# TensorE's matmuls in the order of emission, and background steps every 4 matmuls, in a decoder step

## The chip, the cores and the metric

One core of a Trainium2 chip runs the whole program. The core has TensorE (matmuls; PE in the rows, PEld for its weight loads), VectorE (DVE), ScalarE (ACT), GpSimd (POOL), and SyncE (SP), which issues nearly all DMAs. [...] The metric is the device time of one execution in microseconds.

## The reference

One inference step of a one-layer decoder, for a prompt of 2048 tokens and 8 sample tokens with a cache of 2048 positions each. All arrays are float32.

```python
q, k, v, u = _project(rmsnorm(hp, norm_attn_g[i]), w_in[i])     # 1024 -> 4 x 512
for window, dil in ((128, 1), (512, 4), (2048, 16)):            # dilated windows, 8 heads of 64
    o, l = _dilated_attn_prompt(q, k, v, window, dil)
...
pooled = _pool_mix(u, S, pool_w[i], pool_scale[i])              # trailing means over 2, 4, 8, 16
hp = hp + _mixer_out(outs, lses, pooled, w_out[i])              # merge by exp(lse), then 1024 x 1024
hp = hp + _mlp(hp, norm_mlp_g[i], w_up[i], w_down[i])           # squared ReLU, 1024 -> 4096 -> 1024
hp = hp + _ple(hp, p_prompt[i], ple_norm_g[i], w_ple_gate[i], w_ple[i])
```

The same is computed for the sample tokens, whose attention reads the cache. The outputs are both token groups after a last RMSNorm, the new K and V rows, and the pooling buffers.

## The kernel before

Activations lie transposed, features on the partitions and tokens along the columns. Each dense product is made of groups: `group` (line 340) multiplies a chunk of up to 512 token columns by 128 output features, over 8 blocks of features, into one PSUM bank. Each operand is split into a high and a low part, and three products are summed (`PASSES`), so a group has 24 matmuls (6 in the per-layer embedding, more in the down projection). New weights come by DMA; POOL rounds the high part (`pcopy`, line 199) and DVE subtracts it for the low part (line 196).

The rest of the work, preparing inputs, attention, normalisation, is written as Python generators, called background. A group takes a `hook`; every 12 matmuls and at its end it reports the columns done to a `Pace`, which runs as many background steps as are then due. So instructions of the background are emitted between the matmuls of a group.

The stages, in order: input projection of the first 1024 tokens (columns of 512), while the second half's input is prepared; input projection of the rest (384, 384 and 264 columns) with the first half's attention as background (`Att(0, ...)`), which goes on beside the per-layer embedding product (`ple_mm`); then, for the first 832 tokens (X, chunks of 416), output projection and MLP with the second half's attention (`Att(1, ...)`) and the sample attention (`sample_attn`) as background; then output projection, MLP and gate of the other 1224 tokens (Y, chunks of 416, 416 and 392).

Attention goes head by head. `maxima` finds each query's maximum by masked reductions on DVE (line 776); `units` yields the work of a head in pieces. A unit is: scores into a bank, exponential on ACT (line 868 for the class units of the dilated windows, 871 for the near units of the plain window), two masks on POOL (line 859), a rounding on ACT (line 880), a subtraction on DVE (line 196), then the weighted sums with V. In `out` the sums of a unit are emitted one step after its scores, behind the scores of the next:

```python
for nxt, hold in self.units(h, ops, ov):
    if pend:
        pend()
    pend = nxt
    yield
```

`Stat.finish` sums squares by four one-column matmuls, takes the inverse square root on DVE and ACT (`newton`, line 306), and turns it with four transposes (line 1204). `sample_attn` reads the cache tile by tile; ACT rounds a V tile into one buffer (line 1107), DVE subtracts into another, and two matmuls use them.

The emission order is not the order on the engines. The program is built with `schedule_with_timeline_sim=True`: a scheduler runs a timeline of its own over all emitted instructions and places them on each engine as they come ready in it, earlier emitted ones first. So a matmul of one group can stand between matmuls of another.

Of the kernel before, what the change touches and what calls it, by code (L numbers as in the profile page):

```python
# [147 lines left out]
@with_exitstack  # L148
def decoder_step(ctx: ExitStack, tc: tile.TileContext, I, O):
    nc = tc.nc  # L150
    V, S, G, PE, SP = nc.vector, nc.scalar, nc.gpsimd, nc.tensor, nc.sync
    y_p, y_s, kv_p, kv_s, pool_p, pool_s = O

# [35 lines left out]
    def mm(out, l, r, start, stop):  # L189
        PE.matmul(out, l, r, start=start, stop=stop)  # L190
# [150 lines left out]
    def group(ps, ln, ws, xs, hook=None):  # L341

        n, last, due = 0, 3 * len(ws) - 1, 0
        for w, x in zip(ws, xs):
            for a, b in PASSES:
                mm(ps[:, :ln], w[:, a], x[:, b, :ln], n == 0, n == last)
                n += 1
                if hook and (n % 12 == 0 or n == last + 1):
                    hook((n - due) * ln)
                    due = n  # L350

# [231 lines left out]
    def in_proj(hf, xa, order, rg, mp, tp, hook, ws, first=None):  # L583
# [21 lines left out]
        for ft, ci in [(ft, ci) for ci in range(len(chunks)) for ft in order[:n0]] + [(ft, ci) for ft in order[n0:] for ci in range(len(chunks))]:  # L605
            if ft not in ws:
                ws[ft] = in_w(ft, rg["wr"])
            w, (c0, ln) = ws[ft], chunks[ci]
            if ci and first:
                drain(first)  # L610
                first = None
            ps = mp()
            group(ps, ln, [w[:, :, k] for k in range(KD)], xa.col(ci), first_hook if first else hook)
            now, later = later, []
            later += [x for x in [x() for x in now] if x]
            for o, e, n, lo in pieces(c0, ln):
                if n < 4:
                    if n not in open_:
                        open_[n] = rg["gt"]()
                    tt(V, open_[n][:, lo : lo + e - o], ps[:, o:e], rbc[n][:, lo : lo + e - o], ALU.mult)  # L620
                    if lo + e - o == 512:
                        rest = group_done(ft, n, open_.pop(n), rg, tp)
                        if rest:
                            later.append(rest)
                elif ft >= 12:
                    tt(V, us[:, ft - 12], ps[:, o:e], rbs, ALU.mult)
                    later.append(partial(pool_sample, ft - 12, rg, tp))
                else:
                    t = TINY(NS, key="in", n=2, width=NS)
                    tt(V, t, ps[:, o:e], rbs, ALU.mult)  # L630
                    later.append(sample(ft, t))
# [502 lines left out]
    def ple_mm(mp, tp, wr, pr, hook):  # L1134
# [13 lines left out]
        for c0, ln in ((0, 512), (512, 512), (1024, 512), (1536, 256), (1792, T - 1792)):  # L1148
            pp = pb().rearrange("p (k a c) -> p k a c", a=2, k=2)
            pt = []  # L1150
            for p0 in range(c0, min(c0 + ln, SEQ), 256):
                n, r = p0 // 512, p0 % 512 // P
                t = pr(512).rearrange("p (r d) -> p r d", r=2)
                dma(t, prows[n][:, r : r + 2])
                pt += [(t[:, 0], P), (t[:, 1], P)]
            if c0 + ln == T:
                t = pr(256)[:NS]
                dma(t, I["p_sample"][0].rearrange("b o d -> (b o) d"))
                pt.append((t, NS))
            for k in range(2):  # L1160
                ps = tp()
                for r, (t, rw) in enumerate(pt):
                    PE.transpose(ps[:, r * P : r * P + rw], t[:, k * P : k * P + P], ident[:rw, :rw])
                S.copy(pp[:, k, 0, :ln], ps[:, :ln])
                tt(V, pp[:, k, 1, :ln], ps[:, :ln], f(pp[:, k, 0, :ln]), ALU.subtract)
            for ft in range(KD):
                ps = mp()
                group(ps, ln, [w[ft // 4][:, k, :, (ft % 4) * P : (ft % 4) * P + P] for k in range(2)], [pp[:, k] for k in range(2)], hook)
                o = orr(ln)
                (S.copy if ft % 2 else V.tensor_copy)(o, ps[:, :ln])  # L1170
                dma(ple[ft * P : ft * P + P, c0 : c0 + ln], o)
# [111 lines left out]
    def out_proj(xa, st, dst, wr, hook, acc=None, ring=None):  # L1283
# [11 lines left out]
        for i, (ft, ci) in enumerate(order):  # L1295
            if ft not in ws:
                ws[ft] = load_w(I["w_out"][0][:, ft * P : ft * P + P], KD, wr=wr, ring=ring)
            w = ws[ft]
            c0, ln = chunks[ci]
            ps = mp()  # L1300
            at = (slice(ft * P, ft * P + P), slice(c0, c0 + ln))
            xr = acc[ft].ap[:, c0 - base : c0 - base + ln] if acc else xr_(ln)
            dma(xr, xT[at])
            group(ps, ln, [w[:, :, k] for k in CORDER], [xa[k, ci] for k in CORDER], None if acc and i >= len(order) - 4 else hook)
            tt(V, xr, ps[:, :ln], xr, ALU.add)
            if dst is not None:
                dma(dst[at], xr)
            st.add(ft, ci, xr)
            if done is not None:
                st.finish(done)  # L1310
                done = None
            if ft == KD - 1:
                done = ci
# [249 lines left out]
    hook = Pace(bg, A.steps(), 16 * 24 * 1032 + 0.6 * 48 * T)  # L1563
# [21 lines left out]
    hook = Pace(bg, B.steps(), 24 * NX * (8 + 64 * 0.9))  # L1585
# [122 lines left out]
```

## Time and profile before

| what | value |
|---|---|
| median of 3 runs | 2738.77 us (2737.43 to 2738.94) |
| profiled execution, own time | 2732.91 us |
| its span, first to last instruction | 2731.2 us |
| TensorE busy | 2651.1 us, 97% |
| TensorE weight loads busy | 2526.3 us, 92% |
| DVE, ACT, POOL busy | 57%, 31%, 38% |
| granted TensorE clock, mean | 0.991 |
| DMA, mean | 100 GB/s |

The spans of matmuls overlap, since they are pipelined; a busy TensorE is one that always has a matmul under way. [...]

### The profile page before, as it was taken

The numbers are of one execution on the slowest core, as the hardware profiler recorded it, in microseconds if no ns is written. First come the engines' busy times: TensorE is split into PE (matmuls) and PEld (weight loads), VectorE is DVE, ScalarE is ACT, GpSimd is POOL, SyncE is SP. The second block draws the span as 40 slices with busy tenths as digits, with TensorE's granted clock in tenths as the row PEclk, the third lists the DMA queues.
The fourth block names the chain that finished last, engine by engine and source line by source line (L and its number), as shares of the span: only waits on it lengthen the run. The fifth ranks groups of instructions, "written<-read, shape, count | busy, mean of one in ns | idle before, by whom it ended". The sixth has DMA issues, their size and how long they took to land. (4 is left out here: it accounts for less than half of the span.)

```text
span 2731.2 us, 43094 instructions
## 1 busy us (share of the span) xinstructions
PE 2651.1 (97%) x15686; PEld 2526.3 (92%) x15686; DVE 1559.9 (57%) x3373; ACT 846.6 (31%) x1605; POOL 1030.2 (38%) x1370
## 2 busy tenths in 40 slices
PE   8999999998999999999999898999999999999998
PEld 6888899978988999999999898999999999999997
DVE  6747867675587776775765857432332332332675
ACT  6221445463434134243343424301001011011354
POOL 2415745434385444343344626312112122122263
PEclk9999999999999999999999999999999999999999
DMA  7464345476154233342322545331111111111134
GB/s 248 133 180 124 86 121 136 110 224 177 49 150 113 81 88 82 97 107 71 99 73 66 167 142 149 127 104 39 42 41 42 39 39 39 39 39 39 53 84 150
DMA packets 386194, 272.51 MB, mean 100 GB/s; under 512 B 91722, under 2 KB 349461, under 8 KB 385973
## 3 DMA queue, kind: packets, MB, share of 16 engines
q1 hardware_dynamic: 385397, 269.68, 34.6%
q8 instruction: 123, 2.02, 0.3%
q14 instruction: 90, 0.74, 0.1%
q0 software_dynamic: 512, 0.07, 0.0%
q10 hardware_dynamic: 72, 0.02, 0.0%
HBM read 209.47 MB, written 60.30 MB: 99 GB/s over the span
## 5 line engine op out<-in xcount | busy, mean ns | idle before, releaser
L190 PE MATMUL bank<-mem_r 128*128 128x416 f32 (+11 forms) x13608 | 2454.0, 338 | 46.9 <-DVE mem_r L196 13.3
L190 PEld LDWEIGHTS bank<-mem_r 128*128 128x128 f32 (+2 forms) x13608 | 2307.9, 184 | 127.4 <-DVE mem_r L196 22.9
L199 POOL TENSOR_SCALAR mem_r<-mem_f 128x512 fp32r<-128x512 f32 (+1 forms) x444 | 325.2, 737 | 773.6 <-PE bank L190 689.1
L196 DVE TENSOR_TENSOR mem_r<-mem_f,mem_r 128x512 fp32r<-128x512 f32 (+3 forms) x568 | 435.5, 773 | 176.2 <-POOL mem_r L199 142.8
L196 DVE TENSOR_TENSOR mem_f<-bank,mem_f 128x416 f32<-128x416 f32 (+3 forms) x488 | 272.7, 566 | 234.5 <-PE bank L190 227.6
L196 DVE TENSOR_TENSOR mem_r<-mem_mb,mem_r 128x416 fp32r<-128x416 f32 (+6 forms) x236 | 174.0, 744 | 349.3 <-ACT mem_r L1347 318.3
L1344 ACT ACTIVATE mem_mb<-bank 128x392 f32<-128x392 f32 (+1 forms) x160 | 82.2, 514 | 801.0 <-PE bank L190 801.0
L196 POOL TENSOR_TENSOR mem_mb<-mem_mb 128x416 f32<-128x416 f32 (+1 forms) x140 | 143.7, 1027 | 304.2 <-ACT mem_mb L1344 277.9
L776 DVE CUSTOM_DVE_ANT_0 bank<-bank,mask 128x256 f32<-128x256 f32 (+3 forms) x504 | 159.8, 338 | 33.9 <-PE bank L190 30.1
L199 POOL TENSOR_SCALAR mem_r<-mem_r 128x256 fp32r<-128x256 f32 (+1 forms) x117 | 92.0, 798 | 92.2 <-PE bank L190 81.1
L196 DVE TENSOR_TENSOR mem_ma<-bank,mem_ma 128x416 f32<-128x416 f32 (+2 forms) x104 | 63.4, 610 | 87.5 <-PE bank L190 72.8
L1347 ACT CAST mem_r<-mem_mb 128x416 fp32r<-128x416 f32 (+1 forms) x128 | 68.5, 535 | 134.4 <-POOL mem_mb L196 134.4
L859 POOL TENSOR_SCALAR_AFFINE_SELECT mem_ma<-mem_ma 128x256 f32<-128x256 f32 (+2 forms) x148 | 72.0, 506 | 92.2 <-ACT mem_ma L871 49.3
L190 PE MATMUL bank<-mem_mb,mem_r 128*64 128x64 f32 (+4 forms) x494 | 100.7, 321 | 6.2 <-DVE mem_r L196 2.1
L190 PEld LDWEIGHTS bank<-mem_mb,mem_r 128*128 128x128 f32 (+1 forms) x494 | 78.7, 174 | 16.0 <-POOL mem_r L199 2.8
L196 DVE TENSOR_TENSOR mem_r<-mem_ma,mem_r 128x512 fp32r<-128x512 f32 (+4 forms) x88 | 71.6, 819 | 26.4 <-ACT mem_r L880 20.5
L199 POOL TENSOR_SCALAR mem_r<-mem_mb 128x512 fp32r<-128x512 f32 (+3 forms) x61 | 55.3, 913 | 79.4 <-PE bank L190 55.8
L196 POOL TENSOR_TENSOR mem_f<-mem_f 128x416 f32<-128x416 f32 (+2 forms) x52 | 70.0, 1351 | 31.3 <-DMA mem_f<-in_cache_attn_kv_dram 11.4
L776 DVE DVE_READ_ACCUMULATOR2_ANT mem_ma<- 128x1 f32 (+1 forms) x512 | 68.5, 134 | 0.0
L196 POOL TENSOR_TENSOR mem_ma<-mem_ma 128x416 f32<-128x416 f32 (+1 forms) x41 | 51.8, 1272 | 39.7 <-DMA mem_ma<-h_s 14.1
L196 DVE TENSOR_TENSOR mem_f<-mem_f,mem_ma 128x416 f32<-128x416 f32 (+1 forms) x64 | 46.9, 733 | 26.2 <-ACT mem_ma L1190 11.3
L859 POOL TENSOR_SCALAR_AFFINE_SELECT mem_mb<-mem_mb 128x256 f32<-128x256 f32 (+2 forms) x76 | 34.5, 474 | 57.9 <-ACT mem_mb L868 22.8
(255 smaller groups left out, 1807.7 us busy)
## 6 DMA issues: line engine op xcount, KB each, us to landing
mem_f<-in_w_up_dram SPq DMA_DIRECT2D x128, 256.0 KB
mem_f<-in_w_down_dram SPq DMA_DIRECT2D x128, 256.0 KB
mem_f<-in_w_in_dram SPq DMA_DIRECT2D x64, 256.0 KB
out_dram<-mem_f SPq DMA_DIRECT2D x55, 256.0 KB
mem_f<-in_cache_attn_kv_dram SPq DMA_DIRECT2D x48, 256.0 KB
mem_f<-in_w_ple_gate_dram SPq DMA_DIRECT2D x48, 256.0 KB
mem_f<-in_x_prompt_dram SPq DMA_DIRECT2D x64, 128.0 KB
xT_s<-mem_f SPq DMA_DIRECT2D x32, 256.0 KB
```

What stands on the lines that cost most here:

```text
L190: PE.matmul(out, l, r, start=start, stop=stop)
L196: eng.tensor_tensor(out, a, b, op=op)
L199: G.tensor_scalar(out, src, 1.0, 1.0, op0=ALU.mult, op1=ALU.mult)
L776: V.tensor_tensor_reduce(src, src, mask, 1.0, -3e38, ALU.add, ALU.max, mcol[: src.shape[0], col : col + 1])
L859: G.affine_select(out=p, in_=p, pattern=[[0, nblk], [sign, w]], compare_op=ALU.is_ge, fill=0.0, base=base, channel_multiplier=-sign)
L1344: S.activation(a, ps[:, :ln], AF.Relu)
L1347: S.copy(x[:, 0], sq)
```

## The change

```diff
@@ -148,6 +148,7 @@
 @with_exitstack
 def decoder_step(ctx: ExitStack, tc: tile.TileContext, I, O):
     nc = tc.nc
+    ctx.enter_context(tc.manual_schedule(engines={mybir.EngineType.PE}))
     V, S, G, PE, SP = nc.vector, nc.scalar, nc.gpsimd, nc.tensor, nc.sync
     y_p, y_s, kv_p, kv_s, pool_p, pool_s = O
 
@@ -345,7 +346,7 @@
             for a, b in PASSES:
                 mm(ps[:, :ln], w[:, a], x[:, b, :ln], n == 0, n == last)
                 n += 1
-                if hook and (n % 12 == 0 or n == last + 1):
+                if hook and (n % 4 == 0 or n == last + 1):
                     hook((n - due) * ln)
                     due = n
```

The first edit takes TensorE out of the scheduler's hands: its instructions stand in the order in which the kernel emits them. The other engines are still ordered by the scheduler. The second lets a group report after every 4 matmuls instead of 12, so that the steps due are emitted in smaller lots. All line numbers after the first edit are higher by one.

The order of TensorE's instructions in the two programs differs nearly everywhere. The rows below are TensorE's; `bank_70` to `bank_77` are the eight PSUM banks before, `bank_72` to `bank_79` the same eight after; 128x416 is the matmul's output, x6 the number of equal rows in a run.

First place: a near unit of the second half's attention, first of its head, in the MLP of X. Before, from its four score matmuls (128x256) to the first of its weighted sums (65x256):

```order
L190 MATMUL bank_75<-mem_r 128x256 x4
L190 MATMUL bank_77<-mem_ma_1831 65x64 x8
L190 MATMUL bank_72<-mem_r 128x416 x5
L190 MATMUL bank_70<-mem_r 128x416 x6
L190 MATMUL bank_71<-mem_r 128x416 x6
L190 MATMUL bank_75<-mem_r 128x256 x4
L190 MATMUL bank_73<-mem_r 128x416 x5
L190 MATMUL bank_76<-mem_r 65x256
```

The same unit now:

```order
L191 MATMUL bank_77<-mem_r 128x256 x4
L191 MATMUL bank_79<-mem_ma_1833 65x64 x8
L191 MATMUL bank_73<-mem_r 128x416 x6
L191 MATMUL bank_75<-mem_r 128x416 x4
L191 MATMUL bank_76<-mem_r 128x128 x2
L191 MATMUL bank_78<-mem_r 65x256
```

Between scores and sums stood 22 matmuls of 416 columns and the next unit's scores; now 10 of 416 and two of 128 columns. In the first half's attention the last near unit of a head stands closer still; here that of the fourth head, its scores (bank_77) and sums (bank_79), in the input projection:

```order
L191 MATMUL bank_77<-mem_r 128x256 x2
L191 MATMUL bank_77<-mem_r 128x128 x2
L191 MATMUL bank_73<-mem_r 128x384 x4
L191 MATMUL bank_79<-mem_r 65x256
L191 MATMUL bank_79<-mem_r 64x256
```

One lot of 4 matmuls stands between them. Second place: the weighted sums of one sample token over its three V tiles (16x512, two matmuls for a tile), in the MLP of X. Before:

```order
L190 MATMUL bank_74<-mem_r 16x512 x2
L190 MATMUL bank_71<-mem_r 128x416 x12
L190 MATMUL bank_73<-mem_r 128x416 x10
L190 MATMUL bank_74<-mem_r 16x512
L190 MATMUL bank_73<-mem_r 128x416 x9
L190 MATMUL bank_74<-mem_r 16x512
L190 MATMUL bank_73<-mem_r 128x416 x5
L190 MATMUL bank_75<-mem_r 64x128 x4
L190 MATMUL bank_72<-mem_r 128x416 x5
L190 MATMUL bank_74<-mem_r 16x512
```

And now:

```order
L191 MATMUL bank_72<-mem_r 128x416 x24
L191 MATMUL bank_73<-mem_r 128x416 x4
L191 MATMUL bank_76<-mem_r 16x512 x6
L191 MATMUL bank_73<-mem_r 128x416 x20
L191 MATMUL bank_75<-mem_r 128x416 x8
```

All six stand in one row. Third place: the sums of squares (104x1) and the transposes of the inverse root (128x104) of the first chunk of X, in the output projection. Before:

```order
L190 MATMUL bank_71<-mem_r 128x416 x6
L190 MATMUL bank_72<-ones_96,mem_f 104x1 x4
L190 MATMUL bank_71<-mem_r 128x416 x18
L190 MATMUL bank_73<-mem_r 128x416 x11
L1204 MATMUL bank_72<-ident_91,tiny_7140 128x104 x4
L190 MATMUL bank_73<-mem_r 128x416 x13
```

And now:

```order
L191 MATMUL bank_72<-mem_r 128x416 x24
L191 MATMUL bank_74<-ones_98,mem_f 104x1 x4
L1205 MATMUL bank_74<-ident_93,tiny_7142 128x104 x4
L191 MATMUL bank_73<-mem_r 128x416 x24
L191 MATMUL bank_75<-mem_r 128x416 x24
```

The transposes stood 29 matmuls behind the sums, and now follow them.

## Rows read from the trace of the kernel before

**Rows 1.** The page, part 1: busy us, share of the span and instructions of each engine.

```profile
PE 2651.1 (97%) x15686; PEld 2526.3 (92%) x15686; DVE 1559.9 (57%) x3373; ACT 846.6 (31%) x1605; POOL 1030.2 (38%) x1370
```

**Rows 2.** Waits of TensorE: line, releaser, us in total, times, longest.

```profile
PE bank L190 <- DVE mem_r L196: 15.4, 20, 2.3
PE bank L190 <- DVE mem_f L196: 11.4, 14, 2.9
PE bank L190 <- POOL mem_r L199: 10.8, 8, 2.8
...
PE bank L190 <- ACT mem_r L880: 6.3, 7, 2.4
```

**Rows 3.** Stretches: busy us (instructions) of PE, PEld, DVE, ACT, POOL; clock, DMA, GB/s.

```profile
273.10:341.40 68.30, 62.98 (x439) 58.24 (x440) 56.20 (x155) 28.04 (x52) 49.16 (x61) 0.90 0.32 86
409.70:478.00 68.30, 68.30 (x555) 65.87 (x554) 48.98 (x160) 35.31 (x67) 35.83 (x60) 1.00 0.57 136
614.50:682.80 68.30, 59.23 (x373) 54.74 (x371) 40.48 (x118) 23.65 (x44) 27.63 (x43) 0.90 0.65 177
1911.80:1980.10 68.30, 68.30 (x371) 67.82 (x370) 22.31 (x36) 5.75 (x11) 12.69 (x17) 1.00 0.14 42
```

**Rows 4.** Timeline, start and length in us: a near unit and, in between, the maxima's store.

```profile
449.59 1.11 ACT L871 ACTIVATE mem_ma<-bank 128x512 f32<-128x512 f32 x1
...
450.78 1.21 POOL L859 TENSOR_SCALAR_AFFINE_SELECT mem_ma<-mem_ma 128x256 f32<-128x256 f32 x2 [1.27 <-ACT mem_ma L871]
...
451.55 1.16 PE L190 MATMUL bank<-mem_f 64*65 64x64 f32 x16
...
451.68 1.42 SPq L187 DMA_DIRECT2D m_s<-mem_ma  x3
452.02 0.62 ACT L880 CAST mem_r<-mem_ma 128x512 fp32r<-128x512 f32 x1 [0.39 <-POOL mem_ma L859]
...
452.68 0.69 DVE L196 TENSOR_TENSOR mem_r<-mem_ma,mem_r 128x512 fp32r<-128x512 f32 x1
...
453.49 1.67 SPq L187 DMA_DIRECT2D mem_ma<-m_s  x4
```

**Rows 5.** Lines 868, 859 and 880: count, ns minimum/median/maximum, first and last start.

```profile
L868 ACT ACTIVATE mem_ma<-bank x32: 465/546/602, 277.2 to 1466.3; 128x384 f32<-128x384 f32 x16, 128x512 f32<-128x512 f32 x16
...
L859 POOL TENSOR_SCALAR_AFFINE_SELECT mem_ma<-mem_ma x148: 285/407/1651, 279.1 to 1490.6; 128x256 f32<-128x256 f32 x108, 128x128 f32<-128x128 f32 x24, 64x512 f32<-64x512 f32 x8, 128x512 f32<-128x512 f32 x8
...
L880 ACT CAST mem_r<-mem_ma x64: 510/617/647, 280.3 to 1491.0; 128x512 fp32r<-128x512 f32 x44, 128x384 fp32r<-128x384 f32 x20
```

**Rows 6.** Groups by line and shape, 888 to 1500 us: count | busy us, mean ns.

```profile
L196 DVE TENSOR_TENSOR mem_r<-mem_f,mem_r 128x512 fp32r<-128x512 f32 x127 | 99.5, 788 | 35.7 <-POOL mem_r L199 28.8 <-ACT mem_r L1107 2.7 <-ACT mem_r L880 2.3
...
L1107 ACT CAST mem_r<-mem_f 128x512 fp32r<-128x512 f32 x24 | 14.9, 620 | 44.2 <-PE bank L190 42.7 <-DVE mem_r L196 1.1 <-DMA mem_f<-in_cache_attn_kv_dram 0.4
```

**Rows 7.** Timeline around one finish of the row statistics.

```profile
717.38 0.81 PE L190 MATMUL bank<-ones,mem_f 128*104 128x1 f32 x8
...
720.45 0.16 DVE L196 TENSOR_TENSOR tiny<-tiny,tiny 104x4 f32<-104x4 f32 x1
...
723.62 0.52 PE L1204 MATMUL bank<-ident,tiny 104*128 104x104 f32 x4
```

**Rows 8.** Timeline of TensorE at the start, and the stretch from 10 to 20 us.

```profile
12.90 1.22 PE L190 MATMUL bank<-mem_ma,mem_r 128*128 128x512 f32 x2 [2.84 <-POOL mem_r L199]
...
21.07 1.77 PE L190 MATMUL bank<-mem_ma,mem_r 128*128 128x512 f32 x7
...
26.82 0.60 PE L464 MATMUL bank<-ident,rcols 128*128 128x128 f32 x4
...
10.00:20.00 10.00, 7.16 (x31) 5.56 (x30) 5.93 (x11) 7.51 (x24) 2.50 (x4) 1.00 1.00 316
```

**Rows 9.** Lines 776 and 572: count, ns minimum/median/maximum.

```profile
L776 DVE CUSTOM_DVE_ANT_0 bank<-bank,mask x504: 197/319/469, 232.6 to 1436.6; 128x256 f32<-128x256 f32 x74, 64x128 f32<-64x128 f32 x42, 64x64 f32<-64x64 f32 x37, 128x128 f32<-128x128 f32 x15
...
L572 ACT COPY mem_f<-bank x32: 559/587/652, 39.2 to 551.8; 128x512 f32<-128x512 f32 x32
```

## The prediction

> **What bounds the kernel now.** I read the page's first two parts first, then who TensorE waited for, then stretches of the span, and last the order of rows around the places where the change acts. TensorE is busy for 2651.1 of 2731.2 us [rows 1], so 80.1 us is all that it sits idle; DVE, ACT and POOL are at 57, 31 and 38%. The waits are scattered: 37.6 us of them, the first three rows [rows 2], are mostly for copies and subtractions of freshly loaded weights and for evacuations; waits for attention weights (line 880) come to 6.3 us in seven places. In the dense stretch after 1911.8 us, TensorE runs 371 matmuls of 408 columns on average in 68.3 us [rows 3]: 184 ns each, 0.45 ns a column. I use that price for every matmul of 128 columns or more, and 0.07 us for each of 64 (16 took 1.16 us [rows 4]). The slice from 409.7 us, full of attention and projection, has no idle time either. So before the change TensorE is the bound nearly everywhere, and the order that the scheduler chose hides nearly every chain through the other engines. The most that a better order could give is the 80.1 us and what the clock lost; the loss has no such bound.
>
> **The change, part by part.** No instruction is added or removed; both edits move some. The finer step (4 instead of 12 matmuls) changes where background steps are emitted; in itself it costs nothing, since the same steps come, about one or fewer at a time instead of up to three. The fixed order is what counts: a matmul that waits for ACT, POOL or DVE now holds all matmuls behind it, where before the scheduler put other groups ahead. So I count, at each place, the TensorE work that stands between a result's producer and its consumer (the cover), and set it against the chain through the other engines.
>
> *Attention units.* A unit is scores, exponential, two masks, a rounding, a subtraction, then weighted sums. In one near unit (lines 871 to 881) the exponential starts at 449.59 us, the subtraction ends at 453.37: 3.8 us with almost nothing in front [rows 4]. A class unit: 0.55 + 2 x 0.41 + 0.62 + 0.79, and four handovers of 0.05 to 0.1 us: 3.1 us [rows 5, 6]. The order gives the cover. Over the eight heads of the first half, the four near units had medians of 4.5, 7.1, 8.9 and 8.1 us of matmuls between scores and sums; now 3.2, 1.9, 1.4 and 0.7. In the second half 5.4 to 8.4 us become 2.7, 2.9, 2.4 and 2.1. Of 64 near units two had under 3.6 us, now 61 have. A stall ahead of one unit's sums is cover for the next one's whose scores are already issued. For a head of the first half: 3.8 - 3.2 = 0.6; 3.8 - 1.9 - 0.6 = 1.3; 3.8 - 1.4 - 1.3 = 1.1; the fourth unit's scores come after that, so 3.8 - 0.7 = 3.1: 6.1 us, eight times, 49. The second half: 1.1 + 0 + 1.4 + 1.7 = 4.2, eight times, 34. The same count over the 64 class units gives 10. In all 93 us. With one subtraction of 0.79 us queued in front (chains of 4.5 and 3.9) the same count gives 141. DVE is busy for 49 to 56 us of the 68.3 in such slices [rows 3], so there are gaps, and I stay nearer the lower end: 106 us.
>
> *Sample attention.* For each of eight samples three value tiles pass through one pair of buffers: rounding 0.62 us on ACT, subtraction 0.79 on DVE [rows 6], two matmuls of 0.23 us. The six matmuls stood 10 to 19 dense matmuls apart; now they stand in one row. So the second and third tile each cost about (0.62 + 0.07 - 0.23) + (0.79 + 0.07 - 0.23) = 1.1 us: 16 x 1.1 = 18. The third tile's buffer is refilled by a DMA only after the first is used; no row gives its landing. Lower bound 0; upper, from the store at 451.68 to its read-back at 453.49 us, 1.8 us [rows 4], plus 0.8 for 256 KB at the 316 GB/s of the start [rows 8]: 2.6. I take 1.4, as the subtraction of the second tile covers part: 8 x 1.4 = 11. Together 29.
>
> *Row statistics.* Ten times four sums go through ACT and DVE to four transposes: from the end of the sums at 718.19 us to that of the last DVE step at 720.61, 2.4 us [rows 7]. Some 29 matmuls stood between them, now none: 24 us. Four of the sums now also directly follow the last group whose evacuation, square and addition they need, three operations like those of [rows 5]; I put 1.5 us for what they add, since little else was left to do there before either: 6. Together 30.
>
> *The single transpose bank.* Some 16 transposes of new rows stand right behind others in the same bank and wait for its copy, 0.59 us [rows 9]: 10. Six pooling matmuls stand right behind a POOL copy and a DVE subtraction, about 1.5 us: 9. *Maxima.* The 16 transposes of a head's maxima follow the last reductions, two or more of some 0.32 us and their read-outs [rows 9], about 1.3 us; the cover is 0 to 2.8 us: 9, and 6 where scores wait for a bank. *Per-layer embedding.* Five chunks start with the rounding and subtraction of their own input: about 1.2 us each, 6.
>
> *The start.* Dense matmuls began at 12.9 us, while the statistic of the first rows was ready only for 26.82 us [rows 8]. Now 32 transposes and that statistic come first. 22 matmuls of 512 columns, some 5 us, had been issued by 22.7 us; with the later rows' transposes 6 us are lost. The DMA rate is the bound there, so no more.
>
> *What comes back.* While TensorE stands still the others run ahead: of the 37.6 us of [rows 2] I take back 20. Stalls of different kinds lie among each other: a quarter of the sample, bank and maxima terms, 16.
>
> *The clock.* [...] Attention now gets 8 to 10 us of idle time in each of some 17 slices: 0 to 116 us, of which I take 25, since matmuls at half clock are longer cover for the same chains. [...]
>
> Sum: 106 + 29 + 30 + 19 + 15 + 6 + 6 - 20 - 16 + 25 = 200 us. The profiled execution took 2732.91 us, 1.7 more than its span, and 0.2% under the median of 2738.77; added to the median, 2939, rounded to 2935 us.
>
> **The rivals.**
> *The clock falls in every slice.* For it: the two rows at 0.90; against it: slower matmuls hide more of each chain. With 90 instead of 25: about 3000 us.
> *The stalls hide one another.* Units, samples and statistics share a stretch, the other engines drain their queues in each stall, and what follows finds its input ready. With chains as short as 3.2 and 2.5 us the units cost 62, and half of the rest would remain: about 2850 us.
> *Faster.* Even steps keep the other engines evenly fed, and a fixed order uses results as soon as they stand; then weights come in time and idle time falls to about half: 40 us less, 2700 us. This decides at the near units: the cover has to reach 3.8 us, and the counted covers say 0.7 to 3.2.
> *The order does not bind.* Were TensorE to pass a waiting matmul, nothing would change: 2735 us. Against it: idle time with a single releaser, such as 15.4 us for line 196, while other groups stood behind [rows 2]. [...]
>
> **How the numbers follow.** Forecast (2890 to 2980): 0.46. Clock (2980 to 3060): 0.21. Hidden (2800 to 2890): 0.21. Faster: 0.06. No change: 0.03. Still slower than all: 0.03. Slower by over 0.2%, which is about what a measurement can tell from no change, is then 0.91, the same 0.03, faster 0.06. The range from 2820 to 3050 leaves out the last three and the edges.
>
> **What would show it.** In the profile after, TensorE's first waits should be for line 881 (ACT) and the subtraction of line 197, together 80 to 130 us, and the transposes of line 1205 should wait ten times, about 24 us. Slices in the first half's attention should hold 470 to 510 matmuls instead of 555; slices of the second half's MLP, with no background, should keep 371. The busy sums of DVE, ACT and POOL should stay within 2%. The prediction is wrong if the waits for lines 881 and 197 stay under 40 us, or if TensorE's idle time lies where weights are loaded.

## The result, and the profile after

The changed kernel takes 3078.74 us (median of 4 runs, 3075.49 to 3085.02), the kernel before, run beside it, 2738.86 us: 1.1258 of the time before, with an interval from 1.1243 to 1.1273. The forecast was 2935 us, its range ended at 3050. The direction was right, the size too small by 144 us.

Part 1 of the page after, and the digits of PE and PEclk from part 2 (busy tenths and granted clock in 40 slices):

```profile
span 3073.6 us, 43178 instructions
...
PE 2765.8 (90%) x15686; PEld 2607.6 (85%) x15686; DVE 1553.9 (51%) x3373; ACT 855.9 (28%) x1599; POOL 996.1 (32%) x1370
...
PE   7898688888788999998989959899999999999997
...
PEclk8998889988988999998999989999999999999998
```

Against [rows 1] two things grew, with not one matmul more. TensorE's idle time, span minus busy, went from 80.1 to 307.8 us: 227.7 more. Its busy time went from 2651.1 to 2765.8: 114.7 more, because the same matmuls ran longer. Together 342.4 us, which is the whole difference of the spans (3073.6 - 2731.2). The second part is nearly all the clock: its mean fell from 0.991 to 0.943. The trace's records hold two levels of it, 1.00 and 0.50 of full speed, so that is (1 - 0.943) x 2 x 3073.6 = 350 us at 0.50, where it was about 50 before. Some of that time TensorE was idle anyway. With the trace's records of the granted clock laid over its matmuls, TensorE is busy at the lower level for 255.9 us, against 39.9 before, in 55 stretches against 9. Half of the difference, 108 us of the 114.7, is taken as what the slow clock cost. That is an estimate with twice the time for each matmul at 0.50, and somewhat high: around 2026 us in the trace after, 128x416 matmuls start every 347 ns at 0.50 and every 190 ns at 1.00, so that 45% of their time is lost, which would make it 98 us.

TensorE's longest waits after (line, releaser, us in total, times, longest), to be read against [rows 2]:

```profile
PE bank L191 <- ACT mem_r L881: 77.2, 41, 5.7
PE bank L191 <- DVE mem_r L197: 43.7, 64, 3.1
PE bank L1205 <- DVE tiny L197: 29.5, 10, 7.1
PE bank L191 <- POOL mem_r L200: 26.1, 10, 6.0
PE bank L838 <- DVE mem_ma L777: 22.4, 11, 3.3
PE bank L191 <- DVE mem_f L197: 14.7, 11, 3.4
PE bank L191 <- POOL mem_f L197: 12.2, 1, 12.2
PE bank L465 <- DVE rcols L432: 10.7, 2, 7.1
```

Line 881, the rounding of attention weights, was 6.3 us in seven waits; it is now 77.2 in 41. The same idle time by the shape of the waiting matmul (count | busy us, mean ns | idle before, and what ended it):

```profile
L191 PE MATMUL bank<-mem_r 128*128 128x512 f32 x672 | 186.7, 422 | 35.8 <-POOL mem_r L200 23.0 <-DVE mem_r L197 11.0 <-ACT mem_r L1165 1.3
...
L191 PE MATMUL bank<-mem_r 128*65 128x256 f32 x320 | 91.4, 316 | 105.6 <-ACT mem_r L881 77.2 <-DVE mem_r L197 26.8
...
L191 PE MATMUL bank<-mem_r 128*16 128x512 f32 x48 | 20.8, 461 | 9.9 <-ACT mem_r L1108 5.7 <-DVE mem_r L197 3.7
...
L191 PE MATMUL bank<-ones,mem_f 128*104 128x1 f32 x64 | 8.1, 247 | 14.8 <-POOL mem_f L197 12.2 <-DVE mem_f L197 2.0 <-ACT mem_f L1206 0.7
...
L1205 PE MATMUL bank<-ident,tiny 104*128 104x104 f32 x32 | 6.1, 330 | 22.8 <-DVE tiny L197 22.8
...
L838 PE MATMUL bank<-ident,mem_ma 128*16 128x128 f32 x16 | 4.7, 295 | 22.6 <-DVE mem_ma L777 22.4
...
L1205 PE MATMUL bank<-ident,tiny 98*128 98x98 f32 x8 | 1.8, 384 | 6.6 <-DVE tiny L197 6.6
L191 PE MATMUL bank<-ones,mem_f 128*98 128x1 f32 x16 | 1.7, 228 | 4.7 <-DVE mem_f L197 4.7
```

This view gives one number for each of the larger terms of the prediction: the weighted sums of the attention (128x256 by 65 rows) wait 105.6 us, the maxima's transposes 22.6, the row statistics 22.8 + 6.6 + 14.8 + 4.7 = 48.9, the sample's V products 9.9. The 35.8 us at 128x512 are nearly all at the pooling's products: seven waits for POOL's rounding of the pooled means (23.0), most with one for the subtraction behind it. These are totals after. The attention's sums had 14.0 us in the kernel before, so the change added 92:

```profile
L190 PE MATMUL bank<-mem_r 128*65 128x256 f32 x320 | 85.3, 291 | 14.0 <-DVE mem_r L196 7.3 <-ACT mem_r L880 6.3
```

One such wait in the timeline (start and length in us; in brackets the idle time before and its releaser), the last near unit of a head in the first half:

```profile
363.57 1.51 PE L191 MATMUL bank<-mem_r 128*128 128x128 f32 x5
...
364.73 2.16 POOL L200 TENSOR_SCALAR mem_r<-mem_mb 128x256 fp32r<-128x256 f32 x2 [3.64 <-ACT mem_mb L743]
365.06 0.84 ACT L872 ACTIVATE mem_f<-bank 128x256 f32<-128x256 f32 x2
...
366.86 0.62 POOL L200 TENSOR_SCALAR mem_mb<-mem_mb 128x256 fp32r<-128x256 f32 x1
367.45 0.65 POOL L860 TENSOR_SCALAR_AFFINE_SELECT mem_f<-mem_f 128x128 f32<-128x128 f32 x2
368.13 0.51 ACT L881 CAST mem_r<-mem_f 128x384 fp32r<-128x384 f32 x1 [1.82 <-POOL mem_f L860]
...
368.70 5.34 PE L191 MATMUL bank<-mem_r 128*65 128x256 f32 x18 [3.62 <-ACT mem_r L881]
```

TensorE stands for 3.62 us, though other matmuls are emitted right behind. The exponential is done at 365.90, but the two masks wait on POOL until 367.45, since copies of line 200 lie ahead of them there. The stretches around that wait (columns as in [rows 3]; the wait runs from 365.08 to 368.70):

```profile
357.00:363.80 6.80, 4.69 (x34) 3.92 (x35) 2.67 (x6) 2.21 (x4) 1.02 (x3) 1.00 0.13 43
363.90:365.00 1.10, 1.10 (x4) 0.67 (x3) 0.73 (x3) 1.10 (x3) 0.27 (x1) 0.50 0.00 0
368.70:374.10 5.40, 5.40 (x20) 5.10 (x21) 2.60 (x5) 0.00 (x0) 1.20 (x2) 0.50 0.50 108
374.20:380.90 6.70, 3.65 (x31) 3.44 (x29) 5.26 (x12) 1.46 (x4) 4.73 (x8) 1.00 0.44 102
```

The clock was at its lower level, 0.50, before this wait began. Ahead of the fall, at 1.00, TensorE had been idle for 2.1 of 6.8 us, in shorter waits. It stayed at 0.50 through the wait and through 5.4 us of unbroken matmuls behind it. So time was lost here both in standing, 3.62 us, and in slow matmuls later, 5.4 us of them at 0.50, but the slow matmuls behind one wait need not be that wait's doing.

By stage (columns as in [rows 3]; bounds are the first finish or transpose that opens the next stage):

```profile
0.00:258.00 258.00, 224.06 (x1010) 179.67 (x1010) 137.25 (x266) 78.24 (x223) 64.10 (x124) 0.93 0.52 160
258.00:699.00 441.00, 351.87 (x2444) 326.46 (x2443) 250.81 (x818) 146.54 (x262) 161.12 (x270) 0.89 0.33 88
...
887.00:1831.00 944.00, 841.15 (x4905) 788.65 (x4905) 582.93 (x1258) 311.64 (x529) 392.45 (x524) 0.94 0.30 83
...
1968.00:2928.00 960.00, 945.12 (x5098) 933.83 (x5098) 356.39 (x565) 170.35 (x318) 250.45 (x286) 0.99 0.19 57
```

The same stages of the kernel before took 232.6, 313.8, 824.2 and 954.8 us. The last one, the MLP of Y with no short chain beside its groups, lost 5 us; the two with attention in the background lost 127 and 120. The stages do not hold quite the same matmuls in the two programs: 2444 against 2334 in the first of the two.

### The profile page after: what moved, and what is told of

It reads as the page before. It is cut to its first block, busy times and chain, and to the rows that moved or that the text cites. A ratio compares the mean times of both kernels' runs of the same rounds, so it can differ in the third digit from the quotient of the medians.

```text
span 3073.6 us, 43178 instructions
## 1 busy us (share of the span) xinstructions
PE 2765.8 (90%) x15686; PEld 2607.6 (85%) x15686; DVE 1553.9 (51%) x3373; ACT 855.9 (28%) x1599; POOL 996.1 (32%) x1370
## 5 line engine op out<-in xcount | busy, mean ns | idle before, releaser
L191 PE MATMUL bank<-mem_r 128*128 128x416 f32 (+9 forms) x13608 | 2545.3, 345 | 173.0 <-ACT mem_r L881 77.2
L191 PEld LDWEIGHTS bank<-mem_r 128*128 128x128 f32 (+2 forms) x13608 | 2368.1, 189 | 282.6 <-ACT mem_r L881 88.8
L200 POOL TENSOR_SCALAR mem_r<-mem_f 128x512 fp32r<-128x512 f32 x444 | 310.1, 703 | 909.2 <-PE bank L191 831.1
L197 DVE TENSOR_TENSOR mem_r<-mem_f,mem_r 128x512 fp32r<-128x512 f32 (+5 forms) x568 | 426.8, 756 | 256.5 <-POOL mem_r L200 171.6
L197 DVE TENSOR_TENSOR mem_r<-mem_mb,mem_r 128x416 fp32r<-128x416 f32 (+6 forms) x236 | 167.3, 716 | 384.4 <-ACT mem_r L1348 323.6
L200 POOL TENSOR_SCALAR mem_r<-mem_r 128x256 fp32r<-128x256 f32 (+1 forms) x117 | 83.7, 727 | 151.2 <-PE bank L191 107.3
L860 POOL TENSOR_SCALAR_AFFINE_SELECT mem_ma<-mem_ma 128x256 f32<-128x256 f32 (+2 forms) x148 | 64.2, 455 | 146.3 <-ACT mem_ma L872 73.3
L197 DVE TENSOR_TENSOR mem_r<-mem_ma,mem_r 128x512 fp32r<-128x512 f32 (+4 forms) x88 | 65.0, 738 | 45.1 <-ACT mem_r L881 41.0
L777 DVE DVE_READ_ACCUMULATOR2_ANT mem_ma<- 64x1 f32 (+1 forms) x512 | 68.7, 134 | 0.2
L197 DVE TENSOR_TENSOR mem_f<-mem_f,mem_ma 128x416 f32<-128x416 f32 (+1 forms) x64 | 42.5, 664 | 29.7 <-POOL mem_ma L197 12.2
L860 POOL TENSOR_SCALAR_AFFINE_SELECT mem_mb<-mem_mb 128x256 f32<-128x256 f32 (+2 forms) x76 | 35.5, 487 | 65.3 <-ACT mem_mb L872 26.1
```

The lines of the kernel that those rows point to most:

```text
L197: eng.tensor_tensor(out, a, b, op=op)
L200: G.tensor_scalar(out, src, 1.0, 1.0, op0=ALU.mult, op1=ALU.mult)
L777: V.tensor_tensor_reduce(src, src, mask, 1.0, -3e38, ALU.add, ALU.max, mcol[: src.shape[0], col : col + 1])
L860: G.affine_select(out=p, in_=p, pattern=[[0, nblk], [sign, w]], compare_op=ALU.is_ge, fill=0.0, base=base, channel_multiplier=-sign)
```

## The experiments

All ratios are to the kernel before, run on the same chip beside each group of kernels.

**The two edits apart.** The first edit alone keeps `n % 12`; the second alone leaves out the `manual_schedule` line:

```diff
-                if hook and (n % 4 == 0 or n == last + 1):
+                if hook and (n % 12 == 0 or n == last + 1):
```

> Only the first edit: TensorE in the order of emission, background steps still every 12 matmuls. Theory (the fixed order makes the whole loss; the step size only moves where a unit's sums stand): counted with one chain of 3.8 us, the near units lack about as much cover as in the changed kernel, so 3040 to 3130 us, best guess 3080, with idle time of TensorE near 300 us and a granted clock near 0.94. Rival (the smaller lots make the loss, or most of it): under 2900 us.

> Only the second edit: background steps every 4 matmuls, TensorE still placed by the scheduler. Theory: the scheduler still puts other groups in front of a unit's sums (the order has 3 of 64 near units with under 3.7 us of cover, the kernel before 2), so 2739 us within 10, clock near 0.99. Rival (the smaller lots carry a share of the loss): 2800 us or more.

Measured: the fixed order alone 3112.96 us, ratio 1.1372 (1.1353 to 1.1391); the small steps alone 2731.99 us, ratio 0.9981 (0.9972 to 0.9991). So the fixed order makes the loss, and more than all of it: under it, the smaller lots are worth 34 us (3112.96 to 3078.74). Waits for line 881 in the kernel with the fixed order alone:

```profile
PE 2782.0 (89%) x15686; PEld 2629.6 (84%) x15686; DVE 1554.0 (50%) x3373; ACT 853.5 (27%) x1599; POOL 992.2 (32%) x1370
...
PE bank L191 <- ACT mem_r L881: 88.9, 44, 5.7
```

**More cover for the attention's sums.** In `out`, a unit's sums are emitted a step later, ahead of the scores after the next ones; `LEAD` spreads a head's units evenly:

```diff
-        N_OUT, N_FRONT, N_WAIT, LEAD = 12, 21, 6, 1.8
+        N_OUT, N_FRONT, N_WAIT, LEAD = 13, 21, 6, 1.2
...
-                if pend:
-                    pend()
-                pend = nxt
+                pend.append(nxt)
                 yield
-                if hold:
-                    pend()
-                    pend = None
-            pend()
+                while len(pend) > (0 if hold else 1):
+                    pend.pop(0)()
+            yield
+            for x in pend:
+                x()
```

> The changed kernel, with a unit's weighted sums one background step further behind its scores, and the first half's heads interleaved evenly (factor 1.2 in place of 1.8). By the order, the lack of cover of all attention units against chains of 3.1 and 3.8 us falls from 94 to 23 us. Theory (the loss is stalls at these places, and the clock falls with the idle time): idle time down by about 70 us and, at the proportion of the whole change (228 us idle, 115 us more busy), the busy time down by about 35 as well: 2975 us (2940 to 3010), clock about 0.96. Rival A (the clock has nothing to do with the idle time): busy time unchanged, 3010 us or more. Rival B (the stalls only move to the next wait): 3060 us or more.

Measured: 3033.13 us, ratio 1.1082 (1.1065 to 1.1098), 46 us less than the changed kernel; idle 274.9 us (33 less), busy 2757.0 (9 less). The time is outside the theory's range and inside that of rival A: in the profiled execution hardly any busy time came back by the clock (254.3 us busy at the lower level, 255.9 in the changed kernel). Its waits:

```profile
PE bank L191 <- ACT mem_r L881: 28.8, 15, 4.3
PE bank L191 <- DMA mem_r<-mneg: 27.9, 8, 6.8
...
PE bank L838 <- DVE mem_ma L777: 7.5, 6, 2.0
```

Line 881 fell from 77.2 to 28.8 us and the maxima from 22.4 to 7.5, as the count of cover said. But a wait of 27.9 us came up that was 3.9 before: the transfer of a head's maxima into the score operand (`mneg`), once a head. With even spreading the maxima end right ahead of the next head's scores; the edit itself took away the transfer's cover. Rival B held for this part only, and by a mechanism of the edit, not of the change. In the run with all the edits below, where the first half's maxima end earlier, this wait is 5.4 us.

**Transposes of the row statistics a group later.**

```diff
                 n += 1
+                if n == last + 1:
+                    turn_late()
...
-            ps = self.tp()
-            for i in range(4):
-                PE.transpose(ps[:, i * q : i * q + q], r[:, i : i + 1].to_broadcast([q, P]), ident[:q, :q])
-            S.copy(a, ps[:, :ln])
+            def turn():
+                ps = self.tp()
+                for i in range(4):
+                    PE.transpose(ps[:, i * q : i * q + q], r[:, i : i + 1].to_broadcast([q, P]), ident[:q, :q])
+                S.copy(a, ps[:, :ln])
+
+            late.append(turn)
```

`turn_late` runs what stands in the list `late`, at the end of a group or of a stage.

> The changed kernel, with the four transposes of each row statistic emitted at the end of the next group instead of right behind the sums. Theory: the ten waits of those transposes (29.5 us in the changed kernel) fall to about 5, as six or seven of ten get a group of 2.2 to 4.4 us in front; with the clock some 35 us less: 3045 us (3030 to 3060). Rival (the loss at these ten places is only the next wait's cover): 3070 us or more.

Measured: 3064.75 us, ratio 1.1199 (1.1181 to 1.1217), 14 us less; the transposes' waits fell from 29.5 to 7.0 us, and idle time by 15. The time lies between theory and rival. The loss at these places is real, but some 8 of the 22.5 us came up again at the next sums of squares (14.8 + 4.7 us before, 21.2 + 6.2 now), and the clock gave little back: busy time fell by 1 us (2765.8 to 2764.8), busy time at the lower level by 8 (247.7).

**Work in place of waits.** Ahead of the sums of each near unit stand 12 matmuls more, whose products nobody reads:

```diff
-            def pv_near(b, bl, hi, lo, before, end):
+            def pv_near(b, bl, hi, lo, before, end, ps):
+                for _ in range(12):
+                    mm(ps[:, :256], khl[:, 0, :P], qhh[:, 0, :256], True, True)
...
```

The caller hands over the unit's score bank as `ps`.

> The changed kernel, with 12 added matmuls of 128x256 (row by column products that nobody reads, into the score bank that the exponential has already read) ahead of the weighted sums of each near unit: 64 x 12 = 768 matmuls, 90 us at 0.117 us each. The order then lacks 9 us of cover at near units instead of 85. Theory (the idle time itself pulls the clock down): the added work takes the place of some 75 us of waits for lines 881 and 197, the stretches at half clock fall from 350 to under 250 us and give back 50 us or more: 3045 us (3010 to 3070). Rival (the clock falls for another reason, such as the attention's own small matmuls): half-clock time stays at 320 us or more, and the kernel is at 3085 us or more.

Measured: 3044.58 us, ratio 1.1125 (1.1108 to 1.1141). With 768 matmuls more the kernel is 34 us faster than without them. The page, the waits and the shapes:

```profile
PE 2811.1 (92%) x16454; PEld 2673.4 (88%) x16454; DVE 1566.5 (52%) x3373; ACT 859.3 (28%) x1599; POOL 996.9 (33%) x1370
...
PE bank L191 <- ACT mem_r L881: 9.3, 7, 3.4
...
L191 PE MATMUL bank<-mem_r 128*65 128x256 f32 x320 | 82.1, 291 | 22.1 <-DVE mem_r L197 12.0 <-ACT mem_r L881 9.3
```

Idle time fell by 78 us (307.8 to 229.8). Busy time rose by 45 (2765.8 to 2811.1), where the added matmuls are worth 88 at full clock (768 x 256 columns x 0.45 ns, the prediction's price): the clock gave back some 43. The clock's records agree: 171.5 us busy at the lower level instead of 255.9, which is worth 42 by the same half. The granted mean rose from 0.943 to 0.962, (1 - 0.962) x 2 x 3040.9 = 231 us at 0.50 instead of 350. The 320 matmuls of the sums themselves, which were not touched, take 291 ns each again instead of 316. So with work in place of the standing still the clock fell less here, though the kinds of matmul at these places were the same. The theory's time held; its 50 us or more of clock was a little too much. One thing this run does not separate: the added matmuls take away idle time and add work at once. The next run takes away idle time and adds nothing.

**Every large wait given cover, the order still fixed.** The edits for later sums and for later transposes, and three more: maxima ahead of the preparation of V in the first half too; the statistics at the end of the MLP of X after the next stage's first two groups; the sample's V tiles one to a step, in a bank of their own.

```diff
-            back = [self.maxima, self.prep_v] if self.deep == 1 else [self.prep_v, self.maxima]
+            back = [self.maxima, self.prep_v]
...
-    SAMPLE_STEPS = 21
+    SAMPLE_STEPS = 37
...
                 mm(po[: 2 * H], wb, vl, False, g == 2)
+                if g < 2:
+                    yield
...
-            st.finish(ci)
+            if bychunk:
+                st.finish(ci)
+            else:
+                late.append(partial(st.finish, ci))
...
-    mp = Turns([bank[0], bank[1], bank[3], bank[2]])
+    mp = Turns([bank[0], bank[1], bank[3]])
...
-    bg2 = sample_attn(Turns([bank[4], bank[5]]))
+    bg2 = sample_attn(Turns([bank[2]]))
...
-    bg = prep_norm(from_acc(hx, CX), lambda ci: stx.acc[ci], g_ple, xg, (0, 1))
+    bg = chain(iter([None] * 2), prep_norm(from_acc(hx, CX), lambda ci: stx.acc[ci], g_ple, xg, (0, 1)))
```

> The changed kernel with every large wait given cover and the order still fixed: weighted sums a step later with the heads interleaved evenly, maxima ahead of the preparation of V in the first half too (so that the transfer of the maxima has two steps in front of the first scores), transposes of row statistics a group later, the statistics at the end of the MLP of X after the first two groups of the next stage, and the sample's V tiles one to a step with a bank of their own. Theory (the loss is the sum of these places): sums 105.6 to about 45 us, maxima 22 to 8, statistics 49 to 12, sample 10 to 2, in all 120 us of idle time, and a quarter of that in the clock as in the last runs: 2930 us (2890 to 2970). Rival (stalls move on to the next wait): 2990 us or more.

Measured: 2951.79 us, ratio 1.0787 (1.0771 to 1.0803): 127 us less than the changed kernel. Idle time fell by 88 us to 220.2, busy time by 35 to 2731.1.

```profile
PE 2731.1 (93%) x15686; PEld 2588.5 (88%) x15686; DVE 1561.7 (53%) x3373; ACT 850.1 (29%) x1599; POOL 1003.3 (34%) x1370
...
L191 PE MATMUL bank<-mem_r 128*65 128x256 f32 x320 | 86.2, 303 | 51.2 <-ACT mem_r L889 32.6 <-DVE mem_r L197 17.8
...
L191 PE MATMUL bank<-ones,mem_f 128*104 128x1 f32 x64 | 8.8, 258 | 13.7 <-DVE mem_f L197 6.9 <-POOL mem_f L197 3.5 <-DVE tiny L314 3.2
...
L1216 PE MATMUL bank<-ident,tiny 104*128 104x104 f32 x32 | 5.0, 287 | 2.1 <-DVE tiny L197 1.5 <-ACT mem_f L1217 0.6
L846 PE MATMUL bank<-ident,mem_ma 128*16 128x128 f32 x16 | 4.7, 291 | 11.7 <-DVE mem_ma L785 11.6
...
L191 PE MATMUL bank<-ones,mem_f 128*98 128x1 f32 x16 | 2.3, 267 | 6.2 <-DVE mem_f L197 6.2
L1216 PE MATMUL bank<-ident,tiny 98*128 98x98 f32 x8 | 1.8, 384 | 5.5 <-DVE tiny L197 5.5
```

The theory's range held, with 22 us less gain than its best guess, as 88 us of idle time went instead of 120. The row statistics still wait 13.7 + 2.1 + 6.2 + 5.5 = 27.5 us (12 were expected), the attention's sums 51.2 (45), the maxima 11.7 (8). Of the 35 us of busy time some 26 are the clock by its records and the same half, 29% of the idle time taken away, where a quarter was expected. Even so the kernel with its order made by hand stays 215 us behind the scheduler's, with 220 us of idle time in many small waits.

The runs side by side (TensorE's us in the profiled execution; "given back" is half of what the column before it lacks of 255.9, an estimate as above; the mean clocks are those of all four executions):

| kernel | idle | busy at 0.50 | clock given back | mean clock |
|---|---|---|---|---|
| changed | 307.8 | 255.9 | | 0.940 to 0.944 |
| sums later | 274.9 | 254.3 | 1 | 0.944 to 0.948 |
| transposes later | 292.4 | 247.7 | 4 | 0.940 to 0.948 |
| added matmuls | 229.8 | 171.5 | 42 | 0.959 to 0.962 |
| every large wait covered | 220.2 | 204.8 | 26 | 0.954 to 0.961 |

The two large entries stand clear of the changed kernel in every execution. The 1 and the 4 do not: the mean clock of one kernel varies by up to 0.008. So less idle time brought the clock up where much of it was taken away; whether in proportion is not shown.

**The sample's tiles alone.** The edits of `SAMPLE_STEPS`, the `yield` and the banks from above, by themselves.

> The changed kernel, with the sample attention's V tiles one to a background step (37 steps instead of 21), their sums in a bank of their own (three banks instead of four for the products of the MLP of X). Theory by the trace of the changed kernel: only 9.9 us of waits stand ahead of the 16x512 matmuls, so about 3067 us (3055 to 3079). Rival, the prediction's own term (29 us, with its share of the clock): 3045 us or less.

Measured: 3069.72 us, ratio 1.1209 (1.1188 to 1.1229), 9 us less. The wait ahead of the V products is gone:

```profile
L191 PE MATMUL bank<-mem_r 128*16 128x512 f32 x48 | 15.6, 407 | 2.1 <-DVE so L1099 1.7 <-ACT mem_r L1350 0.3
```

The prediction's 29 us for this place was three times too much, as the trace had said (9.9). The two profiled spans are as good as equal (3074.0 and 3073.6 us), so the 9 us rest on the medians.

**The fixed order from the stages of Y on only.** The `manual_schedule` line stands behind the end of the MLP of X.

> Background steps every 4 matmuls everywhere; TensorE in the order of emission only from the second output projection on (the stages of Y), under the scheduler before that. Theory (each stage loses by its own chains): the three last stages take 137 + 960 + 146 us in the changed kernel and 110 + 955 + 118 in the kernel before, 60 us more, 5 of them in the MLP of Y, whose groups have no short chain beside them: 2732 + 60 = 2792 us (2775 to 2805). Rival (the late stages pay for what the early ones left undone, and lose little by themselves): 2760 us or less.

Measured: 2768.47 us, ratio 1.0115 (1.0093 to 1.0138): 36 us more than the small steps alone, between theory and rival. Idle time is 102.8 us against 78.7, busy time 2665.5 against 2646.4.

```profile
PE bank L190 <- DVE mem_f L196: 19.2, 14, 4.2
PE bank L1204 <- DVE tiny L196: 15.3, 7, 5.1
```

The late stages do lose by themselves, at the transposes of line 1204 (seven waits, 15.3 us, where two had 3.8 under the scheduler) and at evacuations. The 60 us had included the longest wait of line 1205, 7.1 us at the last finish of the MLP of X, and the slow clock behind the 12.2 us for POOL shortly before (a clock of 0.50 from 1820 to 1835 us in the changed kernel, 0.52 from 1831 to 1846); here the scheduler places both. That this makes up the difference to 60 is argued from where the waits lie, not shown by a run.

**The small steps under the scheduler.** Since these alone had come out ahead, steps every 2 and after every matmul (`n % 2`, and no condition), with nothing else changed:

> The kernel before, scheduler and all, with background steps every 2 matmuls instead of 12. If finer lots feed the scheduler's queues more evenly, as steps every 4 gave 0.9981 of the time before: 2725 to 2732 us. If that gain was the chance order of one program: 2732 to 2745 us.

> The kernel before, scheduler and all, with background steps after every matmul. If the finer step is what gave 0.9981 (every 4) and 0.9968 (every 2): 2722 to 2730 us. If those were chance orders of one program: 2730 to 2745 us.

Measured: 2729.39 us, ratio 0.9968 (0.9958 to 0.9979), and 2721.39 us, ratio 0.9944 (0.9929 to 0.9960). With 4, 2 and 1 matmuls to a lot the medians fall each time; the last is the fastest kernel here, 0.6% under the kernel before and just under the range of its theory. The intervals of neighbouring steps overlap, so single steps are not told apart, but all three lie below the kernel before.

```profile
PE 2641.2 (97%) x15686; PEld 2517.9 (93%) x15686; DVE 1561.5 (57%) x3373; ACT 848.8 (31%) x1605; POOL 1032.2 (38%) x1370
```

Its span is 2718.6 us, so 77.4 are idle (80.1 before) and busy time is 10 us less, at a clock of 0.994. Which of the background's steps gain by it was not looked into.

## Why the prediction was right in direction and too small

**The mechanism held.** The first edit alone is slower than both edits, the second alone is not slower at all; TensorE's first waits are for lines 881 and 197 into `mem_r`, 77.2 + 43.7 = 120.9 us, inside the 80 to 130 that were named, and the transposes wait ten times, 29.5 us (about 24 were named).

**The sum of the stalls held, with its parts less so.** Attention units: 106 predicted as added time; ahead of the sums stand 105.6, of which 92 were added. That 106 and 105.6 agree is luck: the plain count had 93, and the 13 on top were for a subtraction queued on DVE, where the wait shown above has a queue on POOL. Row statistics: 30 against 48.9; the four sums were put at 6 and waited 14.8 + 4.7, 12.2 of it once, for POOL's additions at the end of the MLP of X. The pooling's products: 9 against nearly all of 35.8 (3.1 for that shape before). Transposes that wait for a copy of their bank: 10 against 10.0 (lines 592, 523 and 571). Maxima 15 against 22.6. Sample 29 against 9.9. The start 6, against 33.9 us of idle time in the first 258 us (11.0 in the same stage before): 23 more, 12 of them the pooling's. Before any deduction the stall terms added up to 211 us; idle time rose by 227.7.

One price was misread. The trace holds two records for each matmul of 64 columns with float32 operands (16 where the order has eight), so the 1.16 us were eight of them, 0.145 us each and not 0.07. Eight stand ahead of a head's first near sums, whose cover was then counted some 0.6 us too short.

**The step that failed first is the clock**, "0 to 116 us, of which I take 25, since matmuls at half clock are longer cover for the same chains". No run shows the 25 us; in its place the runs show busy time up by 114.7 us, some 98 to 108 of it by the clock (estimates, at 45% and at half of the busy time at 0.50). The reason given for the low value, slower matmuls as cover, was the author's estimate and was not shown as a saving: behind the wait at 368.70 us the clock of 0.50 was paid for 5.4 us of matmuls without a gap. The kernel with added matmuls shows the cause: work in place of idle time at the near units alone gave back some 42 us of clock.

That 114.7 is so near to the upper bound is luck. The bound was 17 attention slices at 6.8 us each, (1.00 - 0.90) x 68.3 us of the two rows at 0.90 [rows 3]. By the clock's records and the same half, the two stages with attention lost 32 + 41 = 73 us; the other 35 lie in stages for which the prediction put nothing. The 6.8 came from the two lowest of nine slices before with more than 5 us of idle time; the others had clocks from 0.95 to 1.00, among them:

```profile
546.20:614.50 68.30, 62.74 (x432) 52.62 (x431) 48.44 (x138) 41.20 (x82) 25.13 (x47) 1.00 0.76 224
2662.90:2731.20 68.30, 56.85 (x358) 54.58 (x356) 37.47 (x64) 28.96 (x51) 22.76 (x25) 0.95 0.48 150
```

The rival with a falling clock was the right one of the four by its mechanism, but it took back the same deductions, so even it ended at 3000; the measured time lies above its range too, in the class that was given 0.03.

**The step that failed second is "What comes back"**, 20 + 16 us. Some 10 did come back. By line it does not show: lines 196 into `mem_f` and 199, 11.4 + 10.8 us in [rows 2], are 14.7 + 26.1 as lines 197 and 200, but 23.0 of the last are the pooling's. By shape the dense groups of 416 columns, before and after, wait half as long:

```profile
L190 PE MATMUL bank<-mem_r 128*128 128x416 f32 x7584 | 1516.4, 354 | 19.3 <-DVE mem_f L196 9.3 <-DVE mem_r L196 4.2 <-ACT mem_ma L1410 2.3
L191 PE MATMUL bank<-mem_r 128*128 128x416 f32 x7584 | 1530.4, 358 | 9.2 <-DVE mem_f L197 4.4 <-DVE mem_r L197 2.1 <-ACT mem_ma L1411 1.7
```

In numbers: 227.7 - (211 - 36) = 53 us of idle time, about half of it the deduction and the rest terms that were put too low, and 114.7 - 25 = 90 us of busy time make up 142 of the 144 us.

**Signs that were off.** The stretch from 409.7 to 478 us was to hold 470 to 510 matmuls and holds 423 (555 before), at a clock of 0.93:

```profile
409.70:478.00 68.30, 57.05 (x423) 53.88 (x422) 34.76 (x128) 25.98 (x46) 22.42 (x41) 0.93 0.34 90
```

POOL's busy time fell by 3.3% (1030.2 to 996.1), not within 2%; DVE and ACT stayed within 1.1%. The MLP of Y kept its rate: 5098 matmuls in 960 us, 5104 in 955 before.

**What stays open.** The near units' chains were counted at 3.8 us; in the one shown, POOL's copies for the next head held up the masks. How much of the 105.6 us is such queueing on POOL was not measured by itself. Whether clock comes back in proportion to the idle time taken away is open too.

## What to carry to other kernels

Here one engine was the bound, and an order that let its instructions pass each other hid far more than the idle time showed (80.1 us with it, 307.8 without). For such a kernel, count, at each chain through other engines, the bound engine's own work between producer and consumer, and price what is lacking as idle time. Then add the clock on top of it, from the rows at its lower level, and do not set it off against the stalls: here the busy time grew by half of what the idle time did (114.7 to 227.7 us). Twelve matmuls without use ahead of each near unit's sums were cheaper than the waits in their place (3044.58 us against 3078.74); work that was due anyway, emitted a step later, did more here where every large wait got it (2951.79 us).

## What the runs showed of the hardware

Unexpected was how little idle time stands ahead of a fall of the clock. Ahead of one, TensorE had stood for 0.37, 1.46 and 0.28 us within 6.8 us at full clock; it then ran at 0.50 from 363.9 to 374.1 us, through a wait of 3.62 us and 5.4 us of unbroken matmuls. 768 matmuls of 128x256 that compute nothing of use made the kernel 34 us faster (3078.74 to 3044.58). By half of the busy time at 0.50 that went, an estimate, the clock gave back 42 us where these matmuls took away 78 us of idle time, and 26 us where 88 us went without any matmul added.
